# Four projections of a two-layer trunk in products of 512 columns instead of twice 256

## The chip, the core and the metric

The kernel runs on one core of a Trainium2 chip. The metric is the device time in microseconds of one execution, the median over repeated runs. The engines are called as the profile calls them: PE (matrix products), PEld (its loads of the stationary operand), DVE (vector), ACT (scalar, activation functions), POOL (GpSimd) and SP (the queue that issues the transfers). A tile is 128 partitions high; PSUM, where PE writes, has eight banks of 512 float32 columns.

## What is computed

The reference is a causal decoder trunk of two layers over 1024 positions of width 1024. Cut to what the change touches:

```python
# layer 0
proj = h @ w_in_even                       # 1024 x 3072: q, f, i, g, u, v, 512 columns each
oa = hgrn2_mix(qa, fa, ia, ga, ...)        # gated linear recurrence, then rmsnorm * silu(g)
ob = gelu(ub) * mixed(layernorm(gelu(vb))) # 128 x 128 causal mixing matrix for each chunk and group
x = x + rmsnorm(concat([oa, ob]) @ w_out_even)
x = x + rmsnorm(square(relu(rmsnorm(x) @ w_ff1)) @ w_ff2)
# layer 1
o = dilated_attention_mix(h, w_in_odd)     # 16 heads
x = x + rmsnorm(o @ w_out_odd)
x = x + rmsnorm(square(relu(rmsnorm(x) @ w_ff1)) @ w_ff2)
```

## The kernel before, in words

Every product is made of three: operands are split into a high part (rounded to the reduced float32 that PE multiplies quickly) and a low part (the rest), and high x high, high x low and low x high are summed in one PSUM bank. `HT` holds the transposed activations, high and low, as 8 blocks of 128 rows (k) by 1024 positions. `WP` is a ring of 12288 words for each partition that holds split weights.

The product in question is `gemm_nat`: for one tile t of 128 positions it takes the 8 k-blocks of `HT` as the stationary operand and streams the weights of the same k-block as the moving operand, so one call is 8 x 3 = 24 matmuls into one bank of the tag `mm`, which has three banks. Before the change the weights come in blocks of 256 columns. `gemm_tr` is the other orientation: weights stationary, 512 positions of `HT` moving.

Weights come in through `load_cols`: for each pair of k-blocks a piece is taken from HBM by SP into one of three small buffers `raw` of 128 x 512 words, ACT copies it into the high half of its place in `WP`, and DVE (in some stages POOL) subtracts to get the low half. A piece is two k-blocks of 256 columns, or one k-block of 512 columns; either way it holds 512 words for each partition.

The stages that matter here:

- Layer 0, recurrence (`hgrn`, heads 0 to 3): long chains of small DVE and ACT steps with small products of PE between them; PE fills the holes with products of later stages.
- Layer 0, block b (gMLP input, the reference's vb): the projection, a gelu of four steps (`gelu2`: ACT, DVE, ACT, DVE), a layer norm (`gmlp_norm`, many tiny DVE steps, then two products on POOL), and four small mixing products with the columns of `vn` as stationary operand (`gmlp_mix`).
- Layer 0, block u (the reference's ub): `gemm_tr` and a gelu, then a product on POOL.
- Layer 0, block g (gate): the projection, tanh, DVE and POOL steps; `onorm` normalises the recurrence's output with many DVE steps on 128 x 4 values; then each tile is transposed into `HT` (`to_HT`, `ob_to_HT`).
- Both layers, output projection (`out_and_ffn`): 8 tiles x 1024 columns. In layer 0 each tile makes all its columns in turn; in layer 1 the first three tiles begin with their first 512 columns, because the last k-block of `HT` is read back from HBM (`reload_oT`) only when the attention ends. Two of the four weight blocks of 256 columns are loaded ahead of the stage, one goes through `WP`, and one, for which `WP` has no room, into four buffers `wide` of 1024 words. The tile is then normalised (`post_part`, `post_end`, `prenorm`) and transposed for the feed-forward.

The order of instructions on each engine is fixed when the kernel is built. The program is written down as a list of operations with the data and buffers that each needs, and `Plan.run` replays it against a table of estimated costs (`cost`, `hop`, `LAG`): whenever an engine is free it takes the earliest-listed operation that is ready by these estimates. Every buffer is assigned in the same replay. So a changed shape also reorders what stands around it. On the chip each engine works through its list in order and waits where an operand isn't there.

## Time and profile before

| | |
|---|---|
| median of 3 runs | 2345.19 us (2344.57 to 2346.19) |
| profiled execution, its own time | 2341.31 us |
| its span, first to last instruction | 2339.5 us |
| PE busy | 2277.3 us (97%), 12466 matmuls |
| DVE, ACT, POOL busy | 1607.7, 1119.3, 1086.5 us |
| mean granted clock of PE | 0.993 |
| matmuls with 256 moving columns | 2688, of which 2304 are in the four projections |

PE busy is the share of the span in which at least one matmul was in the array; matmuls overlap at their ends, so the mean length of one is longer than its share of the time. How quickly a stretch of matmuls goes is read from the start of the first to the start of the next different group. Idle time of PE stands in square brackets behind a row of the timeline, with the engine whose result came last.

### The profile page before, as it was taken

Reading aid. Unit: us, or ns where it says so; the run is one execution under the profiler, and the core shown is the slowest. Engines: PE = TensorE matmul, PEld = TensorE weight load, DVE = VectorE, ACT = ScalarE, POOL = GpSimd, SP = SyncE. Lnnn points to the kernel's source line nnn. Section 1 sums busy time; section 2 is a strip of 40 time slices with the busy share of each in tenths; the row PEclk is TensorE's granted clock in tenths of the full one; section 3 lists DMA queues with packets and bytes.
Section 4 is the critical chain, followed back from the end, with each engine's and each line's share of the span. In section 5 each row is a group of like instructions: output and inputs, shape, how many; then the busy total and the mean of one; then the engine's idle time right before and its main releaser. Section 6 shows DMA issues by size and latency. Waiting matters only on the chain. (4 is left out here: it accounts for less than half of the span.)

```text
span 2339.5 us, 35350 instructions
## 1 busy us (share of the span) xinstructions
PE 2277.3 (97%) x12466; PEld 1996.2 (85%) x12466; DVE 1607.7 (69%) x3146; ACT 1119.3 (48%) x2427; POOL 1086.5 (46%) x1192
## 2 busy tenths in 40 slices
PE   8999999999999998999999999998999999999998
PEld 7888889988888787887999999997988888888887
DVE  7698785565555855848888777876665555777646
ACT  6444435452222343335777777787453222443333
POOL 2121344345555799514555555543245555644204
PEclk9999999999999999999999999999999999999999
DMA  5110114234443867755311111114334444778554
GB/s 172 55 32 24 37 37 132 82 112 168 149 155 133 287 225 250 253 193 173 100 47 46 46 46 46 52 43 140 126 109 149 154 156 140 287 272 297 200 172 161
DMA packets 220921, 319.25 MB, mean 136 GB/s; under 512 B 14132, under 2 KB 111432, under 8 KB 220744
## 3 DMA queue, kind: packets, MB, share of 16 engines
q1 hardware_dynamic: 220744, 317.00, 40.1%
q8 instruction: 98, 1.61, 0.3%
q14 instruction: 79, 0.65, 0.1%
HBM read 226.24 MB, written 90.70 MB: 135 GB/s over the span
## 5 line engine op out<-in xcount | busy, mean ns | idle before, releaser
L422 POOL TENSOR_TENSOR b<-b,b 128x512 f32<-128x512 f32 (+5 forms) x510 | 562.9, 1119 | 715.1 <-ACT b L422 357.0
L422 PE MATMUL mm<-WP,HT 128*128 128x256 f32 (+2 forms) x4704 | 835.1, 324 | 6.9 <-DVE b L422 2.9
L422 PEld LDWEIGHTS mm<-WP,HT 128*128 128x128 f32 x4704 | 713.7, 191 | 50.6 <-DVE b L422 3.3
L422 ACT ACTIVATE b<-b 128x512 f32<-128x512 f32 (+6 forms) x661 | 325.6, 508 | 372.8 <-POOL b L422 200.5
L422 POOL TENSOR_TENSOR b<-b 128x512 f32<-128x512 f32 (+4 forms) x366 | 331.1, 910 | 343.6 <-DVE b L422 233.7
L422 ACT ACTIVATE WP<-b 128x1024 fp32r<-128x1024 f32 (+2 forms) x248 | 194.8, 792 | 345.0 <-PE pb L422 189.3
L422 DVE TENSOR_TENSOR WP<-b,WP 128x1024 fp32r<-128x1024 f32 (+1 forms) x164 | 234.3, 1434 | 145.8 <-ACT WP L422 145.5
L422 DVE TENSOR_TENSOR b<-b,b 128x1024 fp32r<-128x1024 f32 (+6 forms) x371 | 240.3, 664 | 93.4 <-ACT b L422 76.7
L422 ACT ACTIVATE b<-mm 128x512 f32<-128x512 f32 (+3 forms) x362 | 155.0, 441 | 283.4 <-PE mm L422 266.0
L422 DVE TENSOR_TENSOR HT<-b,HT 128x1024 fp32r<-128x1024 f32 (+3 forms) x131 | 189.7, 1456 | 16.8 <-ACT HT L422 16.6
L422 PE MATMUL tr<-b,b 128*128 128x128 f32 x1074 | 172.3, 279 | 24.3 <-DVE b L422 20.0
L422 PE MATMUL pa<-WP,HT 128*128 128x512 f32 x768 | 193.8, 390 | 0.0
L422 DVE TENSOR_TENSOR b<-tr,b 64x128 fp32r<-64x128 f32 (+5 forms) x404 | 162.9, 408 | 33.4 <-ACT b L422 26.1
L422 PE MATMUL tr<-WP,HT 128*128 128x512 f32 x672 | 171.8, 392 | 6.9 <-DVE b L422 6.6
L422 PE MATMUL mm<-HT,b 128*128 128x512 f32 x720 | 174.8, 390 | 1.5 <-ACT b L422 1.5
L422 PE MATMUL pa<-WP,b 128*128 128x512 f32 x720 | 173.6, 389 | 0.8 <-DVE b L422 0.8
L422 ACT ACTIVATE HT<-b 128x1024 fp32r<-128x1024 f32 (+4 forms) x147 | 142.8, 973 | 62.5 <-DMA b<-hc 38.0
L422 PEld LDWEIGHTS pa<-WP,HT 128*128 128x128 f32 x768 | 144.4, 188 | 29.9
L422 PEld LDWEIGHTS tr<-b,b 128*128 128x128 f32 x1074 | 130.1, 148 | 40.5 <-DVE b L422 20.5
L422 DVE TENSOR_TENSOR b<-pa,b 128x512 f32<-128x512 f32 x110 | 75.3, 688 | 129.0 <-PE pa L422 129.0
L422 PEld LDWEIGHTS pa<-WP,b 128*128 128x128 f32 x720 | 135.0, 188 | 29.6 <-DVE b L422 1.6
L422 PEld LDWEIGHTS mm<-HT,b 128*128 128x128 f32 x720 | 134.6, 188 | 29.8 <-ACT b L422 2.3
(63 smaller groups left out, 3074.6 us busy)
## 6 DMA issues: line engine op xcount, KB each, us to landing
b<-in_w_ff_dram SPq DMA_DIRECT2D x172, 512.0 KB, 4.8
hc<-b SPq DMA_DIRECT2D x224, 256.0 KB, 2.1
b<-hc SPq DMA_DIRECT2D x112, 512.0 KB, 5.0
b<-in_w_in_odd_dram SPq DMA_DIRECT2D x64, 192.0 KB, 2.8
x<-b SPq DMA_DIRECT2D x24, 512.0 KB, 2.6
b<-x SPq DMA_DIRECT2D x24, 512.0 KB, 3.3
b<-in_w_in_even_dram SPq DMA_DIRECT2D x32, 256.0 KB, 2.9
wd<-b SPq DMA_DIRECT2D x16, 512.0 KB, 3.2
```

Source lines behind the costliest of these rows:

```text
L422: return getattr(self.real[eng], meth)(*[x.real() if isinstance(x, View) else x for x in a], **{k: x.real() if isinstance(x, View) else x ...
```

## The change

Block b, block g and both output projections are taken in products of 512 columns:

- `gemm_nat` always takes a bank and the weights as they were loaded; one call for 512 columns is 24 matmuls, where two calls of 24 made the same columns.
- Blocks b and g become one entry of the list each (width 512), so their gelu, tanh and gate steps run once on 512 columns. The row sums of the layer norm come out of one accumulation, and the addition of two halves goes.
- The weights of b and g take 8192 words of `WP` each; the next block can be loaded beside them only if it takes at most 4096.
- The output weights are cut by column half and by k: `wout[half, 0]` holds k-blocks 0 to 3 and `wout[half, 1]` holds 4 to 7, 512 columns wide. Layer 0 loads (0, 0) ahead of the stage and (0, 1) into `wide`; (1, 0) and (1, 1) go through `WP` when the gate's weights are done. Layer 1 loads (0, 0) during the last pair of heads and (0, 1) behind it; (1, 1) goes into `wide`.
- `wide` is two buffers of 2048 words instead of four of 1024. Two blocks of SBUF of that size exist.

The number of weight words, pieces and multiplications is the same.

```diff
-    def gemm_nat(self, t, w, c0, width, o=None):
-
-        if o is None:
-            o = self.mm_bank()[:, :width]
+    def gemm_nat(self, t, w, width):
+
+        o = self.mm_bank()[:, :width]
         ts = slice(t * P, (t + 1) * P)
         for k in range(NK):
-            self.mm3(o, self.HT[:, 0, k, ts], self.HT[:, 1, k, ts],
-                     w[0][k][0][:, c0:c0 + width], w[0][k][1][:, c0:c0 + width], k == 0, k == NK - 1)
+            self.mm3(o, self.HT[:, 0, k, ts], self.HT[:, 1, k, ts], *w[k], k == 0, k == NK - 1)
         return o
...
-            blocks = [("b", B0), ("b", B0 + 256), ("u", U0), ("u", U0 + 256), ("g", G0), ("g", G0 + 256)]
+            blocks = [("b", B0, 512), ("u", U0, 256), ("u", U0 + 256, 256), ("g", G0, 512)]
...
-                    self.wout = [self.load_cols(a["w_out_even"][0], [256 * i], 256) for i in range(2)]
+                    self.wout = {(0, 0): self.load_cols(a["w_out_even"][0], [0], 512, (0, 2))}
...
-                        x = self.gemm_nat(t, cur, 0, 256)
+                        x = self.gemm_nat(t, cur[0], 512)
                         if kind == "b":
-                            if half == 0:
-                                sums[t] = self.small(2)
-                            self.gelu2(pl2, vs[t][:, cs], x, accum=sums[t][:, half:half + 1])
-                            if half == 1:
-                                self.gmlp_mix(t, ob, self.gmlp_norm(pl2, vs[t], sums[t]))
+                            s = self.small()
+                            self.gelu2(pl2, vs[t], x, accum=s)
+                            self.gmlp_mix(t, ob, self.gmlp_norm(pl2, vs[t], s))
                         else:
-                            if half == 0:
-                                self.onorm(pl2, oa[t])
-                            th = pl2.tile([P, 256], F32, name="th", tag="th", bufs=2)
+                            self.onorm(pl2, oa[t])
+                            th = pl2.tile([P, 512], F32, name="th", tag="th", bufs=2)
                             nc.scalar.activation(th, x, AF.Tanh, scale=0.5)
                             nc.vector.scalar_tensor_tensor(th, th, 1.0, x, op0=OP.add, op1=OP.mult)
-                            nc.gpsimd.tensor_tensor(oa[t][:, cs], oa[t][:, cs], th, op=OP.mult)
-                            if half == 1:
-                                self.to_HT(t, [oa[t][:, k * P:(k + 1) * P] for k in range(4)], t % 2 == 1)
-                                self.ob_to_HT(t, ob)
+                            nc.gpsimd.tensor_tensor(oa[t], oa[t], th, op=OP.mult)
+                            self.to_HT(t, [oa[t][:, k * P:(k + 1) * P] for k in range(4)], t % 2 == 1)
+                            self.ob_to_HT(t, ob)
...
-                    wnext = self.load_cols_lazy(self.a["w_out_odd"][0], [0], 256)
+                    wnext = self.load_cols_lazy(self.a["w_out_odd"][0], [0], 512, (0, 2))
...
-        self.wout = [wcur, self.load_cols_lazy(self.a["w_out_odd"][0], [256], 256)]
+        self.wout = {(0, 0): wcur, (0, 1): self.load_cols_lazy(self.a["w_out_odd"][0], [0], 512, (4, 6))}
...
-            self.wout.append(self.load_cols(wo, [512], 256))
-            self.wout.append(self.load_cols(wo, [768], 256, buf=[
-                pl.tile([P, 1024], F32R, name="wide", tag=f"wide{j}", bufs=1) for j in range(4)]))
+            wide = [pl.tile([P, 2048], F32R, name="wide", tag=f"wide{j}", bufs=1) for j in range(2)]
+            for x in ((0, 0), (0, 1), (1, 0), (1, 1)):
+                if x not in self.wout:
+                    buf = wide if x == ((1, 1) if l else (0, 1)) else None
+                    self.wout[x] = self.load_cols(wo, [512 * x[0]], 512, (4 * x[1], 4 * x[1] + 2), buf)
...
-                bank = self.mm_bank()
-                for i in range(2):
-                    self.gemm_nat(t, self.wout[2 * hf + i], 0, 256, bank[:, 256 * i:256 * i + 256])
+                bank = self.gemm_nat(t, self.wout[hf, 0][0] + self.wout[hf, 1][0], 512)
```

Three places of the built order bear on the prediction. In these rows a name with a number (`b_541`) is a block of SBUF that the planner handed out, so the numbers differ between the kernels; `mm`, `tr`, `pa`, `pb` are PSUM tags.

**PE at the end of the recurrence.** `pb` rows read the recurrence out, `tr` rows with a right operand such as `b_569` are its state updates, and `mm<-WP,HT` is block b's projection. Before:

```order
L422 MATMUL tr<-b_86,b_349 128x128 x4
L422 MATMUL pb<-b_541,b_230 128x128
L422 MATMUL pb<-b_93,b_431 128x128
L422 MATMUL tr<-b_93,b_569 128x128 x2
L422 MATMUL pb<-b_686,b_230 128x128
L422 MATMUL pb<-b_93,b_431 128x128
L422 MATMUL pb<-b_686,b_230 128x128
L422 MATMUL pb<-b_94,b_431 128x128
L422 MATMUL tr<-b_94,b_569 128x128
L422 MATMUL pb<-b_541,b_230 128x128
L422 MATMUL pb<-b_94,b_431 128x128
L422 MATMUL mm<-WP,HT 128x256 x228
```

and with the change:

```order
L422 MATMUL mm<-WP,HT 128x512 x3
L422 MATMUL tr<-b_93,b_569 128x128 x2
L422 MATMUL mm<-WP,HT 128x512 x6
L422 MATMUL pb<-b_686,b_230 128x128
L422 MATMUL pb<-b_93,b_431 128x128
L422 MATMUL pb<-b_686,b_230 128x128
L422 MATMUL pb<-b_94,b_431 128x128
L422 MATMUL tr<-b_94,b_569 128x128
L422 MATMUL mm<-WP,HT 128x512 x6
L422 MATMUL pb<-b_541,b_230 128x128
L422 MATMUL pb<-b_94,b_431 128x128
L422 MATMUL mm<-WP,HT 128x512 x33
```

Block b's matmuls now stand between the recurrence's last steps; between the recurrence's last use of `WP` for its own weights and its last read-out stand 69 of 512 columns, where 72 of 256 stood.

**DVE at the end of block u.** `SCALAR_TENSOR_TENSOR` rows with `mm` are the gelu steps that free a bank, `WP<-` rows are the last step of a weight piece, 128x4 rows belong to `onorm`. Before, the gate's first four pieces end among the earlier gelus of u:

```order
L422 TENSOR_TENSOR WP<-b_87,WP 128x512
L422 SCALAR_TENSOR_TENSOR b_2733<-b_2618,mm 128x512
L422 TENSOR_SCALAR b_86<-b_86 128x4
L422 TENSOR_TENSOR b_89<-b_86,b_89 128x4
L422 TENSOR_TENSOR WP<-b_88,WP 128x512
L422 TENSOR_TENSOR b_89<-b_86 128x4
L422 TENSOR_TENSOR WP<-b_89,WP 128x512
```

With the change the last four of the gate's eight pieces stand behind the last step of u's seventh gelu (the first row) and, the eighth, behind that of its eighth (the row ahead of the last):

```order
L422 SCALAR_TENSOR_TENSOR b_2655<-b_2344,mm 128x512
L422 TENSOR_TENSOR b_94<-b_94,b_86 128x512
L422 TENSOR_TENSOR WP<-b_88,WP 128x512
L422 TENSOR_TENSOR WP<-b_89,WP 128x512
L422 TENSOR_TENSOR WP<-b_87,WP 128x512
L422 SCALAR_TENSOR_TENSOR b_2447<-b_2447,mm 128x512
L422 TENSOR_TENSOR b_86<-b_89,b_86 128x4
L422 TENSOR_TENSOR b_89<-b_86 128x4
L422 TENSOR_TENSOR b_89<-b_89,b_86 128x4
L422 TENSOR_SCALAR b_89<-b_89 128x4
L422 SCALAR_TENSOR_TENSOR b_2447<-b_2447,mm 128x512
L422 TENSOR_TENSOR WP<-b_88,WP 128x512
```

The gate's last weights are now ready only when block u's gelus are over.

**PE where layer 1's attention ends.** The last `pb` rows are the last products of the attention, `mm_74` to `mm_76` are the three banks, so a change of the number is a change of tile or column half. Before:

```order
L422 MATMUL pb_81<-b8_8892,b15_8796 128x128 x2
L422 MATMUL mm_76<-WP_67,HT_63 128x256 x9
L422 MATMUL mm_74<-WP_67,HT_63 128x256 x21
L422 MATMUL mm_75<-WP_67,HT_63 128x256 x27
L422 MATMUL mm_76<-WP_67,HT_63 128x256 x27
L422 MATMUL mm_74<-WP_67,HT_63 128x256 x27
```

and with the change:

```order
L422 MATMUL pb_81<-b1_8060,b15_7964 128x128 x2
L422 MATMUL mm_76<-WP_67,HT_63 128x512 x21
L422 MATMUL mm_75<-WP_67,HT_63 128x512 x9
L422 MATMUL mm_74<-WP_67,HT_63 128x512 x3
L422 MATMUL mm_76<-WP_67,HT_63 128x512 x3
L422 MATMUL mm_75<-WP_67,HT_63 128x512 x15
L422 MATMUL mm_74<-WP_67,HT_63 128x512 x12
```

Before, 30 matmuls of 256 columns stand between the attention's last product and the first that needs the last k-block of `HT`; now 30 of 512 columns do, and the first that needs it are the three of `mm_74`.

More of the change, by code (lines that the diff above doesn't have):

```diff
@@ L886, in layer0_mix @@
                         nxt = (self.load_cols(w, [Q0 + (h + 1) * P, F0 + (h + 1) * P], P) if h < 3
-                               else self.load_cols(w, [blocks[0][1]], 256))
+                               else self.load_cols(w, [blocks[0][1]], blocks[0][2]))
                     state = self.hgrn(ph, h, b, fps, qps, oa, state)
@@ L893, in layer0_mix @@
             pl2 = nc.pool(2)
-            pl2.reserve("gz256", 256, F32, 2)
             vs = [pl2.tile([P, 512], F32, name="vs", bufs=NT) for t in range(NT)]
             ob = [[pl.tile([P, 2, 512], F32, name=f"ob{i}{j}") for j in range(2)] for i in range(2)]
-            sums = {}
-            for n, (kind, c0) in enumerate(blocks):
+            for n, (kind, c0, width) in enumerate(blocks):
                 nxt = None
                 if n + 1 < len(blocks):
-                    nxt = self.load_cols(w, [blocks[n + 1][1]], 256)
+                    nxt = self.load_cols(w, [blocks[n + 1][1]], blocks[n + 1][2])
                 else:
-                    self.wout = [self.load_cols(a["w_out_even"][0], [256 * i], 256) for i in range(2)]
-                half = n % 2
-                cs = slice(half * 256, half * 256 + 256)
-                if n == 2:
+                    self.wout = {(0, 0): self.load_cols(a["w_out_even"][0], [0], 512, (0, 2))}
+                if n == 1:
                     pl2.__exit__()
@@ L914, in layer0_mix @@
                             self.gelu2(pl2, u, x)
-                            o = ob[hf][half][:, j]
+                            o = ob[hf][n - 1][:, j]
                             nc.gpsimd.tensor_tensor(o, o, u, op=OP.mult)
@@ L962, in gmlp_norm @@
         mu = self.small(nm="mu")
-        nc.vector.tensor_tensor(mu, sums[:, 0:1], sums[:, 1:2], op=OP.add)
-        nc.vector.tensor_scalar(mu, mu, -1.0 / 512, None, op0=OP.mult)
+        nc.vector.tensor_scalar(mu, sums, -1.0 / 512, None, op0=OP.mult)
         vn = pool.tile([P, 512], F32, name="vn", tag="vn", bufs=3)
@@ L1187, in qkv_stream @@
         self.rawp = self.cp, "raw", 3, [[nc.vector], [nc.vector, nc.gpsimd], [nc.vector, nc.vector, nc.gpsimd], [nc.gpsimd]][LAG["tail"]]
-        self.wout = [wcur, self.load_cols_lazy(self.a["w_out_odd"][0], [256], 256)]
-        for x in self.wout:
+        self.wout = {(0, 0): wcur, (0, 1): self.load_cols_lazy(self.a["w_out_odd"][0], [0], 512, (4, 6))}
+        for x in self.wout.values():
             for _ in x[2]:
@@ L1406, in out_and_ffn @@
                         next(weights0, None)
-            self.wfree(*self.wout[:3])
+            self.wfree(*self.wout.values())
         self.rawp = self.cp, "raw", 3, [nc.vector]
```

2 lines of the change are left out of this document (1 added, 1 removed).

## The prediction

> **What bounds the kernel now.** I read the page's first part, then the instruction groups by shape, then the timeline of PE, and last the table of stretches where PE pauses.
>
> ```profile
> PE 2277.3 (97%) x12466; PEld 1996.2 (85%) x12466; DVE 1607.7 (69%) x3146; ACT 1119.3 (48%) x2427; POOL 1086.5 (46%) x1192
> ...
> L422 PE MATMUL mm<-WP,HT 128*128 128x256 f32 x2304 | 300.9, 288 | 6.4 <-DVE b L422 2.9 <-ACT HT L422 1.5 <-DVE HT L422 1.4
> ...
> L422 PE MATMUL mm<-b,HT 128*128 128x256 f32 x384 | 50.4, 285 | 0.0
> ```
>
> PE is busy for 97% of the span, so its own work sets the time nearly everywhere, and only 62 us in all are left to pauses. The 256-column matmuls number 2304 + 384 = 2688. Of these 2 x 8 x 24 = 384 belong to layer 0's value input, which stays as it is. The other 2304 are what the change touches: 384 each in blocks b and g, 768 in each output projection. The means of 288 and 285 ns can't be used as a price, because neighbouring matmuls overlap; the price is the time from start to start:
>
> ```profile
> 232.25 27.61 PE L422 MATMUL mm<-WP,HT 128*128 128x256 f32 x228 [1.63 <-DVE b L422]
> 259.70 1.06 PE L422 MATMUL tr<-b,b 128*128 128x128 f32 x8
> ...
> 296.38 29.53 PE L422 MATMUL mm<-HT,WP 128*128 128x512 f32 x129
> 325.75 5.91 PE L422 MATMUL mm<-WP,HT 128*128 128x256 f32 x48
> 332.96 23.30 PE L422 MATMUL mm<-WP,HT 128*128 128x256 f32 x192 [1.30 <-DVE b L422]
> 356.11 0.60 PE L422 MATMUL tr<-b,b 128*128 128x128 f32 x4
> ...
> 1762.79 2.88 PE L422 MATMUL pa<-WP,b 128*128 128x512 f32 x12
> 1765.51 2.88 PE L422 MATMUL pb<-WP,b 128*128 128x512 f32 x12
> ```
>
> 256 columns: (259.70 - 232.25)/228 = 120.4 ns and (356.11 - 332.96)/192 = 120.6 ns. 512 columns: (325.75 - 296.38)/129 = 227.7 ns and (1765.51 - 1762.79)/12 = 226.7 ns. Twice the columns cost 1.89 times as much, so a fixed part of about 14 ns goes with each matmul.
>
> **The matmuls (term 1).** 2304 matmuls of 256 columns become 1152 of 512. Each pair gains 2 x 120.5 - 227.2 = 13.8 ns, together 1152 x 13.8 = 15.9 us: 5.3 in blocks b and g (384 pairs), 10.6 in the output projections (768 pairs). With the one or the other 512-column row the term is 15.3 or 16.5 us. For the output projection the table of stretches (busy us and instructions of PE, PEld, DVE, ACT, POOL, then granted clock and DMA) has
>
> ```profile
> 395.00:495.00 100.00, 100.00 (x782) 96.80 (x781) 58.84 (x121) 43.56 (x112) 31.17 (x23) 1.00 0.23 84
> ```
>
> PE without a pause and DVE at 59%: nothing else comes near, so the 10.6 us should arrive whole.
>
> The Trainium skill ("TensorE: Matmul & The Clock Gate", section "Back-to-back issue gap") gives a warm gap of N/2.4 + 2.5 ns, which speaks against the change: by it a pair would gain 2.5 ns, and my estimate from it is 1152 x 2.5 = 2.9 us. The rows above have a fixed part five times that size, and the measurement decides.
>
> **The pauses of layer 0's blocks (term 2).** The same table:
>
> ```profile
> 206.50:233.00 26.50, 22.10 (x169) 20.25 (x168) 20.49 (x60) 10.22 (x33) 2.60 (x2) 1.00 0.09 27
> 233.00:260.00 27.00, 27.00 (x227) 27.00 (x227) 15.05 (x60) 10.84 (x26) 2.59 (x2) 1.00 0.13 39
> 260.00:310.00 50.00, 46.25 (x270) 39.86 (x270) 49.09 (x192) 24.99 (x89) 25.80 (x20) 1.00 0.13 39
> 310.00:336.00 26.00, 24.70 (x144) 21.77 (x143) 25.86 (x88) 9.37 (x28) 13.94 (x11) 1.00 0.16 51
> ```
>
> PE pauses 4.40 us at the end of the recurrence, nothing in the first half of b, 3.75 in b's second half and u, and 1.30 at the third group of g: 9.45 us. The reason is the third column. While b's first half is multiplied DVE is 56% busy, because only the gelu can be done; with the second half the layer norm and the mixing come on top and DVE is 98 to 99% busy until 336 us.
>
> The change spreads this. A bank now holds 24 matmuls of 512 columns, so the three `mm` banks hold 16 us of filler for the recurrence's end instead of 8.7. In the order 69 matmuls of 512 stand where 72 of 256 stood, 15.7 us instead of 8.7; the 7 us more are work moved forward into the holes. And each tile's layer norm can begin after its one projection, from the start of b.
>
> Whether DVE keeps up decides how much is kept:
>
> ```profile
> L422 DVE SCALAR_TENSOR_TENSOR b<-b,mm 128x256 f32<-128x256 f32 x31 | 12.8, 416 | 10.4 <-ACT b L422 10.2
> L422 DVE SCALAR_TENSOR_TENSOR b<-b,mm 128x512 f32<-128x512 f32 x16 | 10.8, 678 | 0.1
> L422 DVE TENSOR_TENSOR b<-b 128x4 f32<-128x4 f32 x46 | 10.8, 248 | 0.1
> L422 DVE TENSOR_TENSOR b<-b,b 128x4 f32<-128x4 f32 x26 | 8.1, 322 | 0.0
> L422 DVE TENSOR_TENSOR b<-b 128x1 f32<-128x1 f32 x23 | 7.9, 351 | 0.2
> ```
>
> DVE's work from 233 to 336 us is 15.05 + 49.09 + 25.86 = 90 us. Block b's 32 gelu steps of 416 ns become 16 of 678, which takes off 32 x 416 - 16 x 678 = 2.5 us; about 87 are left. By the order the first gelu steps stand ahead of the recurrence's last state updates, so they start at about 230 us, and DVE is through with u at about 317 if it never waits. PE for itself would start g at 325.75 - 4.40 - 3.75 - 192 x 0.0138 = 315 us. It needs the gate's last weight piece 21 matmuls later, at 315 + 21 x 0.227 = 319.8; that piece stands in DVE's order behind u's last gelu step, so it comes at about 318. The two meet with 2 us to spare. The third group of g, which had to wait before, now starts at 315 + 48 x 0.227 = 326, long after its bank is free.
>
> I take 3 us of pauses left (the mixing products that wait for POOL, and short gaps in the recurrence) and so a gain of 6.5 us. Bounds: all 9.45 gone; or DVE 6 us later than above, which puts about 4 us of waiting at the gate's weights beside the old pauses at the recurrence, 3 more than before on balance.
>
> **Layer 1's entry into the output projection (term 3).**
>
> ```profile
> 1606.55 4.01 PE L422 MATMUL mm<-WP,HT 128*128 128x256 f32 x30
> 1612.06 14.55 PE L422 MATMUL mm<-WP,HT 128*128 128x256 f32 x105 [1.50 <-ACT HT L422]
> 1629.32 3.04 PE L422 MATMUL mm<-WP,HT 128*128 128x256 f32 x24
> ...
> 1637.96 2.68 PE L422 MATMUL mm<-b,HT 128*128 128x256 f32 x21
> 1642.83 0.74 PE L422 MATMUL tr<-b,b 128*128 128x128 f32 x4 [2.19 <-DVE b L422]
> ```
>
> After the attention's last product 30 matmuls cover the way of the last k-block into `HT`, 5.5 us, and PE waits 1.50. The 30 are now twice as wide, 6.8 us, so this wait should go but for some tenths at the second tile. The wait of 2.19 us is different: the first tile's last matmul ends at 1629.3, its transposes start at 1642.83, so its normalisation takes 13.5 us. Between the two stand 93 matmuls of 256 columns now and 51 of 512 then, 11.2 and 11.6 us: it gets 0.4 us shorter. I take 1.5 us together; bounds 0 and 3.69.
>
> **Weights that come later.** In layer 0 eight pieces instead of four go through `WP` after the gate is done. Their pace before:
>
> ```profile
> 381.41 0.63 ACT L422 ACTIVATE b<-b 128x512 fp32r<-128x512 f32 x1 [2.25 <-DMA b<-in_w_out_even_dram]
> 383.41 0.63 ACT L422 ACTIVATE b<-b 128x512 fp32r<-128x512 f32 x1 [0.88 <-DMA b<-in_w_out_even_dram]
> 385.25 0.63 ACT L422 ACTIVATE b<-b 128x512 fp32r<-128x512 f32 x1 [0.15 <-DMA b<-in_w_out_even_dram]
> 386.21 0.63 ACT L422 ACTIVATE b<-b 128x512 fp32r<-128x512 f32 x1 [0.33 <-DMA b<-in_w_out_even_dram]
> ```
>
> (386.21 - 381.41)/3 = 1.6 us each, 2.0 at worst. Three wait in the `raw` buffers and go in as the gate's k-blocks come free, the third some 2.7 us before the gate's last matmul; the other five take 8 to 10 us, so the last is there 7 to 9 us after that matmul, counting ACT and DVE. PE needs it after the first column half (24 x 0.227 = 5.4) and seven eighths of the second (4.8), 10.2 us after. Cost nothing, cover 1 to 3 us; without the cover it costs what is missing, up to 3 us. The two large `wide` buffers hold the same four pieces as the four small ones. In layer 1 the first of them is needed 63 matmuls of 512 columns after the attention's last product, 14.3 us, where it was 135 of 256, 16.3 us; PE didn't wait for it, so it costs 0 to 2 us, and I take 0. In the feed-forward I put nothing.
>
> **The sum.** 15.9 + 6.5 + 1.5 = 23.9 us off the profiled execution's own 2341.31 us is 2317.4. The median of the runs shown, 2345.19, is 3.9 above that execution, so the forecast for the median is 2321.
>
> **The rivals.**
>
> *The pauses stay.* DVE ran at 98 to 99% where PE paused, and its work hardly falls; it may only be shifted. Against it: 12 us of DVE idle in 233 to 260 become usable. Time: 2345.2 - 15.9 = 2329, and 2332 to 2334 if the gate's weights come 3 to 5 us late.
>
> *DVE eats all of layer 0's part.* Only the output projections gain: 2345.2 - 10.6 = 2334.6, up to 2340 with more waiting at u. It needs DVE 8 us or more behind my 317.
>
> *Slower: DVE and POOL in each other's way.* The same small operation takes 0.15 or 1.25 us:
>
> ```profile
> 304.34 1.25 DVE L422 TENSOR_TENSOR b<-b 128x4 f32<-128x4 f32 x1
> ...
> 306.72 0.15 DVE L422 TENSOR_TENSOR b<-b 128x4 f32<-128x4 f32 x1
> ```
>
> It happens while POOL works. The layer norms now run beside POOL from b's first tile on. Today's extra over 0.15 in the three groups of 46, 26 and 23 above is 4.5 + 4.5 + 4.6 = 13.6 us. If all 95 waited 1.1 us, 104 us, DVE would end u at 317 + 91 = 408 and the third group of g would start 82 us late: 2403. It turns the change into a loss (over 2349.9) once DVE ends u after 354.5, 0.4 us more on each of the 95. POOL's work is the same as before, which speaks against it. The Trainium skill ("SBUF — State Buffer", section "Who interferes with whom") says that a DVE instruction with two SBUF inputs contends with a POOL instruction that reads SBUF; these rows agree.
>
> *The change doesn't do what it says.* If the fixed part went with the columns, 512 would cost 241 ns and nothing would be gained; with a fixed part of 2.5 ns the gain is 2.9 us, 2342. The rows with 129 and 12 matmuls speak against both.
>
> **How the numbers follow.** Chances: the forecast (2316 to 2327) 0.55; the pauses stay (2327 to 2334) 0.27; DVE eats layer 0's part (2334 to 2340) 0.08; below 2316, with nearly all pauses gone, 0.05; no fixed part gained 0.03; slower 0.02. A measurement of this kernel can tell about 0.2%, 4.7 us, from no change; so faster 0.95, same 0.03, slower 0.02. The range 2315 to 2332 holds the forecast, the upper bounds of terms 2 and 3 short of their last 2 us, and most of the first rival.
>
> **What would show it.** Right: 512-column groups of `mm<-WP,HT` at 227 ns from start to start, 10.9 us of products for one tile of an output projection (48 x 0.227; 96 x 0.1205 = 11.6 before), no PE pause at the third group of g, DVE near 90% busy from the first tiles of b on, less than 4 us of PE pauses between the recurrence's end and g's end, no wait of 1.50 us in layer 1. Wrong: a pause of several us at g's first group (weights) or at u's groups (banks), waits of the first output tile for weights, or new pauses in the feed-forward, where I expect no difference.

## The result and the profile after

The changed kernel takes 2320.35 us (median of 4 executions, 2318.44 to 2320.78) where the kernel before took 2344.88 (median of 4, 2340.43 to 2346.19): ratio 0.9901, 95% interval [0.9889, 0.9913]. Timed once more later it took 2319.14 us (2317.92 to 2319.7) beside 2342.86 of the kernel before: 0.9893 [0.9878, 0.9909]. The forecast was 2321.0. In the four later comparisons the kernel before had medians of 2342.35, 2342.72, 2342.86 and 2343.83, so the 2345.19 that the forecast started from lay high, and the gain is 22 to 25 us.

The profiled execution has a span of 2318.9 us (2339.5 before), an own time of 2320.68, and a mean clock of 0.995. The page's first part and the instruction group by shape that the change made:

```profile
PE 2259.9 (97%) x11314; PEld 1929.9 (83%) x11314; DVE 1616.1 (70%) x3106; ACT 1114.1 (48%) x2403; POOL 1097.3 (47%) x1184
...
L422 PE MATMUL mm<-WP,HT 128*128 128x512 f32 x1824 | 455.5, 394 | 1.7 <-DVE b L422 1.2 <-DVE HT L422 0.5
```

1152 matmuls fewer, and DVE, ACT and POOL nearly as before. That the total came out right says little about the terms, so here is the same point of the program in both PE timelines (start of the named row, us):

| point | before | after | gained in the stage |
|---|---|---|---|
| last gate and query products of the recurrence | 205.03 | 203.70 | 1.33 |
| first product of block g | 325.75 | 314.91 | 9.51 |
| first product of layer 0's feed-forward | 475.21 | 463.57 | 0.80 |
| first transposes of layer 1's normalisation | 1079.87 | 1065.63 | 2.60 |
| last product of the attention | 1605.26 | 1591.35 | -0.33 |
| first product of layer 1's feed-forward | 1708.42 | 1689.40 | 5.11 |
| end of the last matmul | 2332.00 | 2311.05 | 1.93 |

The first 1.33 us are not the change: PE's first instruction stands at 9.37 us before and 8.24 after, and executions of these kernels differ there by about a microsecond. The other rows come from one execution of each kernel. In a second profiled execution of the changed kernel (e11 below) the same stages differ from these by 0.0, 0.2, 0.6, 0.3, 0.7 and 0.0 us, so a few tenths mean nothing. Block b and u gained what was forecast; the gate and layer 0's projection together, where 9.25 us were expected (2.65 + 5.3 of products and the pause of 1.30), gained 0.80; and both feed-forwards, where nothing was expected, gained 4.5.

**Block b to block g.** The PE timeline after, where g begins:

```profile
314.91 9.68 PE L422 MATMUL mm<-WP,HT 128*128 128x512 f32 x42
327.60 0.66 PE L422 MATMUL tr<-b,b 128*128 128x128 f32 x4 [3.00 <-POOL b L422]
328.01 7.33 PE L422 MATMUL mm<-WP,HT 128*128 128x512 f32 x24
...
335.53 5.73 PE L422 MATMUL mm<-WP,HT 128*128 128x512 f32 x24
```

and the table of stretches from the recurrence's end to g (busy us and instructions of PE, PEld, DVE, ACT, POOL, then granted clock and DMA):

```profile
205.00:231.50 26.50, 26.01 (x152) 22.20 (x151) 20.57 (x57) 9.60 (x27) 2.57 (x2) 1.00 0.10 29
231.50:268.80 37.30, 35.80 (x184) 29.09 (x183) 31.61 (x121) 15.79 (x41) 15.81 (x12) 1.00 0.03 8
268.80:315.00 46.20, 45.81 (x210) 37.74 (x209) 46.20 (x174) 24.81 (x86) 21.55 (x17) 1.00 0.25 74
```

At the recurrence's end 0.49 us of pause are left of 4.40, in b and u 1.50 + 0.39 of 3.75. DVE is 85% busy in b and has no gap in u. The stage's gain of 9.51 us is 2.65 of products and 5.77 of pauses (8.15 before, 2.38 after); the remaining 1.1 us are not accounted for. Then there are two things that the kernel before did not have: PE waits 3.00 us for POOL ahead of the gate's first transposes, and the 24 matmuls behind them take 7.33 us, while the next 24 take 5.73. The clock says why. Microsecond by microsecond, after the pause:

```profile
328.00:329.00 1.00, 1.00 (x7) 0.87 (x6) 1.00 (x3) 0.60 (x1) 0.16 (x1) 0.95 0.00 0
329.00:330.00 1.00, 1.00 (x4) 0.69 (x4) 0.97 (x2) 0.00 (x0) 1.00 (x1) 0.50 0.64 225
...
332.00:333.00 1.00, 1.00 (x5) 0.78 (x5) 0.00 (x0) 0.00 (x0) 1.00 (x1) 0.84 0.81 227
```

The granted clock (third number from the right) drops to 0.50, for the three microseconds from 329 to 332: 0.05 + 3 x 0.50 + 0.16 = 1.7 us are lost after the pause, on top of it.

**Layer 0's output projection**, the transposes of four neighbouring tiles in the PE timeline, without the products between them:

```profile
411.53 0.66 PE L422 MATMUL tr<-b,b 128*128 128x128 f32 x4 [0.75 <-DVE b L422]
...
424.30 0.66 PE L422 MATMUL tr<-b,b 128*128 128x128 f32 x4 [0.75 <-DVE b L422]
...
435.70 1.03 PE L422 MATMUL tr<-b,b 128*128 128x128 f32 x8
...
447.48 1.04 PE L422 MATMUL tr<-b,b 128*128 128x128 f32 x8
```

The undisturbed tile takes 447.48 - 435.70 = 11.78 us (12.38 before); three tiles take 12.76, because DVE ends the tile's normalisation 0.75 us late. DVE's last step of it is a pair of 512-element multiplications. Its timeline, and POOL's, in a tile that waits and in one that doesn't:

```profile
408.98 2.49 DVE L422 SCALAR_TENSOR_TENSOR b<-b,b,b 128x512 f32<-128x512 f32 x2
...
434.51 1.42 DVE L422 SCALAR_TENSOR_TENSOR b<-b,b,b 128x512 f32<-128x512 f32 x2
```

```profile
409.65 1.27 POOL L422 TENSOR_TENSOR b<-b,b 128x512 f32<-128x512 f32 x1 [4.15 <-ACT b L422]
...
435.24 3.08 POOL L422 TENSOR_TENSOR b<-b,b 128x512 f32<-128x512 f32 x2 [4.22 <-ACT b L422]
```

The pair takes 2.49 us where POOL's operation on the next column half begins inside it and is through first, and 1.42 where POOL is the one that takes longer. Before, the pair took 1.41 to 1.42 us in these tiles (407.18, 419.56). So 1.07 us are lost to the two engines in each other's way. Which of them waits hangs on little: POOL's operation begins 0.67 us into the pair in the slow tile and 0.73 us into it in the other. This is read from the trace; no run takes POOL's operation away.

**Layer 1's entry** lost its wait at the last k-block but got others; and where the kernel before waited 1.50 us, its clock fell too. The PE timeline after, and then two of the stretches behind that wait before:

```profile
1624.89 1.42 PE L422 MATMUL tr<-b,b 128*128 128x128 f32 x8 [3.45 <-DVE b L422]
...
1642.48 0.66 PE L422 MATMUL tr<-b,b 128*128 128x128 f32 x4 [0.93 <-DVE b L422]
...
1661.90 0.66 PE L422 MATMUL tr<-b,b 128*128 128x128 f32 x4 [0.75 <-DVE b L422]
```

```profile
1612.00:1613.00 1.00, 0.94 (x4) 0.82 (x5) 0.39 (x1) 0.00 (x1) 0.00 (x0) 0.77 0.75 215
1613.00:1614.00 1.00, 1.00 (x7) 1.00 (x6) 0.05 (x1) 0.71 (x2) 0.00 (x0) 0.50 0.94 277
```

From 1612 to 1617 us the granted clock before was 0.77, 0.50, 0.50, 0.52 and 1.00: in this execution that wait cost 1.50 + 1.7 us. After the change the first tile's transposes wait 3.45 us for DVE. Here are the 15 us ahead of them, in which that tile is normalised, and the 20 us behind:

```profile
1610.00:1625.00 15.00, 11.55 (x52) 9.26 (x51) 10.72 (x21) 11.51 (x23) 2.93 (x2) 1.00 0.47 145
1625.00:1645.00 20.00, 19.07 (x87) 15.32 (x88) 19.12 (x37) 13.32 (x31) 5.17 (x3) 0.91 0.43 146
```

DVE is 71% and ACT 77% busy ahead of the transposes, and DVE 96% behind them. Both also write the reloaded halves into `HT` there, between the steps of the normalisation, so what the transposes wait for looks like a chain over two engines and not like DVE at its limit.

**The feed-forward's first weights.** SyncE's queue before and after:

```profile
467.11 12.72 SPq L422 DMA_DIRECT2D x<-b  x2
...
496.26 0.94 SPq L422 DMA_DIRECT2D b<-in_w_ff_dram  x2
```

```profile
456.77 2.30 SPq L422 DMA_DIRECT2D b<-in_w_ff_dram  x4
```

The first loads into `ff1`'s landing buffers `R` are issued at 496.3 us before and 456.8 after. The blocks that the planner gives the buffers in the built kernels suggest why; e2 and e3 below test it. `R` needs blocks of 2048 words, and there are two. Four `wide` buffers of 1024 words go into small blocks; `ff1`'s first weights (`unit0`, 4 x 1024 words) are then put into the two large ones, and `R` waits until they are used up. Two `wide` buffers of 2048 take the large blocks, `unit0` goes elsewhere, and `R` follows `wide`, which in layer 0 is free after the last tile's first column half. Three PE waits are gone after the change, in layer 0 and alike in layer 1; these are the rows before:

```profile
508.74 3.01 PE L422 MATMUL mm<-HT,b 128*128 128x512 f32 x12 [0.74 <-ACT b L422]
...
514.70 2.60 PE L422 MATMUL pa<-WP,b 128*128 128x512 f32 x10 [0.45 <-DVE b L422]
...
524.73 3.02 PE L422 MATMUL pa<-HT,b 128*128 128x512 f32 x12 [0.63 <-DVE b L422]
```

### The profile page after: what moved, and what is told of

The parts are those of the page before. It is cut to its first block, busy times and chain, and to the rows that moved or that the text cites. A ratio compares the mean times of both kernels' runs of the same rounds, so it can differ in the third digit from the quotient of the medians.

```text
span 2318.9 us, 32947 instructions
## 1 busy us (share of the span) xinstructions
PE 2259.9 (97%) x11314; PEld 1929.9 (83%) x11314; DVE 1616.1 (70%) x3106; ACT 1114.1 (48%) x2403; POOL 1097.3 (47%) x1184
## 4 chain that ended last, share of the span: by engine, by line
PE 75%; DVE 12%; ACT 4%; POOL 3%; DMA 3%; issue 2%; SPq 0%; DVEq 0%; ACTq 0%; POOLq 0%
PE mm L422 34%; PE pa L422 20%; PE pb L422 13%; PE tr L422 9%; DVE b L422 9%; POOL b L422 3%; ACT b L422 3%; DVE WP L422 2%; DVE HT L422 1%; DMA b<-in_w_ff_dram 1%; DMA b<-in_w_in_odd_dram 1%; DMA b<-oTd 1%; DMA b<-hc 1%; ACT HT L422 0%; ACT WP L422 0%
## 5 line engine op out<-in xcount | busy, mean ns | idle before, releaser
L422 POOL TENSOR_TENSOR b<-b,b 128x512 f32<-128x512 f32 (+4 forms) x500 | 576.4, 1169 | 668.3 <-ACT b L422 324.5
L422 PE MATMUL mm<-WP,HT 128*128 128x512 f32 (+2 forms) x3744 | 822.5, 362 | 3.3 <-DVE HT L422 1.2
L422 PEld LDWEIGHTS mm<-WP,HT 128*128 128x128 f32 x3744 | 655.3, 190 | 82.1 <-DVE HT L422 2.3
L422 DVE TENSOR_TENSOR WP<-b,WP 128x1024 fp32r<-128x1024 f32 (+1 forms) x164 | 225.8, 1385 | 127.9 <-ACT WP L422 127.5
L422 DVE TENSOR_TENSOR HT<-b,HT 128x1024 fp32r<-128x1024 f32 (+3 forms) x131 | 217.9, 1671 | 23.2 <-ACT HT L422 23.0
```

The costliest lines, as they stand in the source:

```text
L422: return getattr(self.real[eng], meth)(*[x.real() if isinstance(x, View) else x for x in a], **{k: x.real() if isinstance(x, View) else x ...
```

## The experiments

All times are medians; "the changed kernel" stands for 2320.35 us. The kernel before took 2342.35 us beside the first four runs, 2342.72 beside the next four, 2342.86 beside the next three and 2343.83 beside the last. Rows are from the PE timeline where nothing else is said.

**Two halves for each matmul (e1).** In `gemm_nat`:

```diff
-            self.mm3(o, self.HT[:, 0, k, ts], self.HT[:, 1, k, ts], *w[k], k == 0, k == NK - 1)
+            for c in range(0, width, 256):
+                self.chain3(o[:, c:c + 256], self.HT[:, 0, k, ts], self.HT[:, 1, k, ts],
+                            w[k][0][:, c:c + 256], w[k][1][:, c:c + 256],
+                            k == 0 and c == 0, k == NK - 1 and c == width - 256)
```

> The changed kernel (2320.35 us) with each of its 1152 matmuls of 512 columns issued as two of 256 columns on the same weights, banks and order of tiles; the result is the same. Theory (a fixed part of 13.8 ns goes with each matmul): 1152 x 13.8 = 15.9 us come back on PE, less up to 3 us of them where PE now waits for the first gate tile and for three output tiles, so 2333 to 2336 us; two neighbouring 256-column matmuls 241 ns from start to start. Block b stays ordered tile by tile, so the pauses at the recurrence's end and in b stay gone. Rival 1 (a fixed part of 2.5 ns): 2323 us. Rival 2 (the pauses went because of the width itself): they come back, 2342 us.

Measured: 2331.91 us (2330.5 to 2333.2), 11.6 more than the changed kernel. Layer 0's projection:

```profile
440.71 0.60 PE L422 MATMUL tr<-b,b 128*128 128x128 f32 x4
...
453.11 0.60 PE L422 MATMUL tr<-b,b 128*128 128x128 f32 x4
```

A tile takes 12.40 us again, 0.62 more than the undisturbed 11.78, which is 12.9 ns for each of its 48 pairs. Layer 1's projection costs 4.82 us more (12.6 ns for each of 384 pairs), though PE's waits in it are 0.4 us shorter; without that it would be about 13.7 ns. So the fixed part goes with the matmul and is about what the prediction said; a fixed part of 2.5 ns would have given 0.12 us per tile. The total came out 1 us under the range. No tile of layer 0 waits for DVE now, which the range allowed for, and the pauses up to block g got shorter too. They did not return: from the last gate and query products to block g PE pauses 1.7 us (2.4 in the changed kernel, 8.2 before), and the stretch is only 1.3 us longer than in the changed kernel. Wide matmuls are not what removed them.

**Block b in two column passes again (e5).** `blocks` begins with `("b", B0, 256), ("b", B0 + 256, 256)`, with the sums and the layer norm split as before.

> The changed kernel with block b back at twice 256 columns, the first column half over all tiles and then the second, as before; u, g and both output projections as changed. Theory (the pauses went because each tile's layer norm now follows its one projection, from the start of b): the pauses at the recurrence's end and in b's second half and u come back, 8.15 us where the changed kernel has 2.3, and the products cost 192 x 13.8 ns = 2.6 more; the gate starts 8 to 9 us later and the time is 2328 to 2330 us. Rival (the pauses went because three banks hold 16 us of filler): the filler is halved, but DVE's order alone is not decisive, 2323 to 2325 us.

Measured: 2328.4 us (2326.99 to 2331.43). Block g:

```profile
323.54 9.68 PE L422 MATMUL mm<-WP,HT 128*128 128x512 f32 x42
336.57 1.11 PE L422 MATMUL tr<-b,b 128*128 128x128 f32 x4 [3.35 <-POOL b L422]
```

The gate starts 8.63 us later than in the changed kernel, as the theory said, and the first waits of b and u are those of the kernel before (1.07, 0.48, 0.92 us). Counted from the last gate and query products of the recurrence and set beside e1: 256 columns tile by tile cost the gate's start 1.3 us, 256 columns in two passes 8.3. So it is not the width. The order of the tiles, by which each layer norm follows its one projection, and the longer filler that three banks hold then, both come back with e5 and both stay with e1; these runs don't tell the two apart.

**The gate in two passes again (e4).** `blocks` ends with `("g", G0, 256), ("g", G0 + 256, 256)`, with tanh, gate steps and transposes split as before.

> The changed kernel with block g back at twice 256 columns, all else as changed. Products: 192 x 13.8 ns = 2.6 us more. Theory 1 (the wait of 3.00 us at the gate's first transposes and the 1.6 us behind it come from asking for a tile's transposes at once, and two passes of 256 give DVE and POOL 23 us to get there): 4.6 us less, 2318.4 us in all. Theory 2 (DVE comes out of block u at 318 us and is late whatever stands next, so the wait moves to the fourth group of g, which needs a bank that DVE frees at about 325): the wait stays 2 to 4 us, 2321 to 2323 us.

Measured: 2319.76 us (2318.28 to 2320.6), no difference from the changed kernel.

```profile
316.00 5.91 PE L422 MATMUL mm<-WP,HT 128*128 128x256 f32 x48
322.16 23.30 PE L422 MATMUL mm<-WP,HT 128*128 128x256 f32 x192 [0.26 <-DVE b L422]
```

The wait of 3.00 us and the half clock behind it are gone, and what is left in their place is 0.26. From g to the feed-forward the kernel is 0.99 us faster than the changed one: 4.6 for the pause less 2.65 for the products and one more of the 0.98 us tiles. So in block g the change won nothing: what the wide matmuls gained went into a pause that the single pass had opened.

**The gate's transposes two tiles later (e6).** Shortened; the two tiles left in `late` are transposed behind the loop.

```diff
                         x = self.gemm_nat(t, cur[0], 512)
+                        if len(late) == 2:
+                            self.to_HT(*late.pop(0))
...
-                            self.to_HT(t, [...], t % 2 == 1)
+                            late.append((t, [...], t % 2 == 1))
```

> The changed kernel with one thing moved: in block g a tile's transposes stand two tiles later in the program, so PE has 72 matmuls of 512 columns (16.3 us) ahead of the first of them instead of 42 (9.5 us). Theory (the 3.00 us wait and the 1.6 us lost behind it are a wait for the gate's first product on POOL, which ends at 327.5 us): both go, 4.6 us less, 2315.8 us. Rival (DVE and POOL are late in any case, so PE waits for the bank of the first tile at the fourth, or for the output projection's first weights): 2319 to 2320 us.

Measured: 2317.23 us (2315.43 to 2317.67).

```profile
315.44 16.49 PE L422 MATMUL mm<-WP,HT 128*128 128x512 f32 x72
331.76 0.60 PE L422 MATMUL tr<-b,b 128*128 128x128 f32 x4
```

No pause and no half clock; the stage from g to the feed-forward is 4.42 us shorter (4.6 expected). Of these, 3.7 are left at the end of the profiled execution and 3.1 in the median. Against the changed kernel's second measurement (2319.14 us) it is 1.9 in the median. As ratios to the kernel before, the two intervals overlap (0.9891 [0.9878, 0.9905] and 0.9901 [0.9889, 0.9913]), so the gain is clear in the stage and not in the total.

**Large extra buffers alone (e2).** In the kernel before:

```diff
-            self.wout.append(self.load_cols(wo, [768], 256, buf=[
-                pl.tile([P, 1024], F32R, name="wide", tag=f"wide{j}", bufs=1) for j in range(4)]))
+            wide = [pl.tile([P, 2048], F32R, name="wide", tag=f"wide{j}", bufs=1) for j in range(2)]
+            self.wout.append(self.load_cols(wo, [768], 256, buf=[x[:, i:i + 1024] for x in wide for i in (0, 1024)]))
```

> The kernel before (2344.88 us) with one thing of the change alone: the projection's four extra weight pieces lie in two buffers of 2048 words instead of four of 1024. No matmul changes. Theory (found in the two traces, not in the prediction): the feed-forward's landing buffers R need blocks of 2048 words, of which there are two; with small extra buffers the feed-forward's first weights sit there and the first R load is issued at 496 us, while with large ones R follows the extra weights and is loaded some 20 us earlier. The PE waits of 0.74, 0.45, 0.63 us (layer 0) and 0.74, 0.34, 0.63 us (layer 1) behind the feed-forward's start go: 3.5 to 4 us, so 2341 us. Rival (the waits come from DVE and ACT being busy, the loads have nothing to do with it; the prediction's own view): no change, 2345 us.

Measured: 2342.5 us, ratio 0.9998 [0.9989, 1.0007]. The six waits did go: the stage from layer 0's feed-forward to layer 1 is 3.74 us shorter, from layer 1's feed-forward to the end 2.63. But layer 1's output projection became 5.0 us longer:

```profile
1612.16 14.53 PE L422 MATMUL mm<-WP,HT 128*128 128x256 f32 x105 [3.52 <-ACT HT L422]
...
1644.55 1.97 PE L422 MATMUL tr<-b,b 128*128 128x128 f32 x8 [3.47 <-DVE b L422]
```

Both waits were there before, with 1.50 and 2.19 us. A new one of 0.51 us stands at 1605.92, and behind the second the clock is 0.50 for about seven microseconds instead of three, which is 1.4 us more. R's loads moved as the theory said, from 496.26 to 474.47 us in layer 0 and from 1729.51 to 1709.49 in layer 1. The mechanism was right and the time was not: it was lost at another place, which I hadn't priced. In layer 1 the large blocks hold the attention's last buffers; that the extra weights come later for that reason was not tried by itself.

**Four small buffers in the changed kernel (e3).**

```diff
-            wide = [pl.tile([P, 2048], F32R, name="wide", tag=f"wide{j}", bufs=1) for j in range(2)]
+            wide = [pl.tile([P, 1024], F32R, name="wide", tag=f"wide{j}", bufs=1) for j in range(4)]
```

(each k-block's high and low half then lie in one of them).

> The changed kernel with the extra weights in four buffers of 1024 words again, all else as changed. Theory (early R loads are worth 3.5 to 4 us): the waits behind the start of both feed-forwards come back, 2324 us. Rival (the size of the buffers is worth nothing, as predicted): 2320.4 us. A wait of the first output tile of layer 0 for weights is possible beside it, since the small blocks come free later: up to 2 us more.

Measured: 2321.79 us (2319.78 to 2322.05), 1.4 more, about as much as two measurements of the changed kernel differ (2320.35 and 2319.14). The waits returned in both layers:

```profile
497.38 3.01 PE L422 MATMUL mm<-HT,b 128*128 128x512 f32 x12 [0.69 <-ACT b L422]
...
1722.59 3.01 PE L422 MATMUL mm<-HT,b 128*128 128x512 f32 x12 [0.74 <-ACT b L422]
```

From layer 1's feed-forward to the end it takes 1.78 us more, as the theory wants. Layer 0's projection also waits 0.23 and 0.73 us for weights at 376 and 378 us, as the expectation had allowed. Layer 0's feed-forward is 2.28 us behind after its first 400 matmuls and has made it up by layer 1: in the second half of the feed-forward PE waits in every one of these kernels, mostly for DVE, 1.85 + 7.30 + 1.20 us in the changed kernel and 0.53 + 2.70 + 2.35 + 1.38 here. Why that stall got shorter I did not find. By the traces the large buffers are worth 1 to 2 us here, less than the forecast of this run; the medians don't tell that from the 0 of the prediction.

**The projections' transposes later (e7), and both (e8).** Behind two column halves in layer 0 and three in layer 1 (shortened; `turn_in` does what the line taken out and the two behind it did):

```diff
                 bank = self.gemm_nat(t, self.wout[hf, 0][0] + self.wout[hf, 1][0], 512)
+                late = [x - 1 for x in late]
+                if late and late[0] <= 0:
+                    late.pop(0)
+                    turn_in(done.pop(0))
...
-                    self.h_to_HT(t, ys[t])    # and ff1_sums, weights0
+                    late.append(3 if l else 2)
+                    done.append(t)
```

> The changed kernel with the transposes of a finished tile of the output projections moved later: behind two column halves of the next work in layer 0 (48 matmuls, 10.9 us, where 33 stand now) and behind three in layer 1 (72, 16.3 us, where 51 stand). Theory (the waits of 0.75 us in layer 0, each with some 0.2 us beside it, and of 3.45, 0.93 and 0.75 us in layer 1 are the normalisation of a tile being 8 and 15 us long): they go, 2.9 + 5.1 us, 2312.3 us. Rival (the wait only moves to the feed-forward, whose sums of two tiles come later): 2317 to 2320 us.

Measured: 2322.03 us (2318.89 to 2322.4). The rival was right:

```profile
401.73 1.03 PE L422 MATMUL tr<-b,b 128*128 128x128 f32 x8
413.50 1.04 PE L422 MATMUL tr<-b,b 128*128 128x128 f32 x8
...
474.69 0.66 PE L422 MATMUL tr<-b,b 128*128 128x128 f32 x4 [0.51 <-DVE HT L422]
...
1639.16 1.97 PE L422 MATMUL tr<-b,b 128*128 128x128 f32 x8 [5.45 <-DVE HT L422]
```

In layer 0 every tile now takes 11.8 us and the projection is 3.08 us shorter, but the feed-forward, whose first transposes come out of the sums of tiles 6 and 7, is 3.04 longer. In layer 1 the wait moved some 13 us back and grew: 72 matmuls and not 51 stand ahead of it, and PE still waits for DVE.

> The changed kernel with the transposes moved later in block g (two tiles) and in both output projections (two and three column halves). Theory: the gains add, 4.6 + 8.0 us, 2307.7 us, faster than both kernels. Rival (what is gained is waited for in the feed-forward, where PE has pauses of some 10 us for DVE already): 2313 to 2318 us.

Measured: 2317.12 us (2315.49 to 2318.6), the same as with the late gate alone.

**Only tiles 0 to 4 of layer 0 later (e9), and the reload on POOL (e10).** e9 is e6 with e7's late list for tiles 0 to 4 of layer 0 alone (`if l or t > 4: turn_in(t)`, else two column halves later); e10 adds one line in `reload_oT`:

```diff
-        (nc.gpsimd if t < LAG["rel"] else nc.vector).tensor_tensor(lo, src, hi.bitcast(F32), op=OP.subtract)
+        (nc.gpsimd if t >= 4 else nc.vector).tensor_tensor(lo, src, hi.bitcast(F32), op=OP.subtract)
```

> The changed kernel with the gate's transposes two tiles later (the edit that gave 3.1 us) and, in layer 0's output projection alone, the transposes of tiles 0 to 4 later by two column halves; tiles 5 to 7, whose sums the feed-forward waits for, and layer 1 stay as changed. Theory (the 3 us that the late transposes of both layers gained in layer 0 were lost again in the feed-forward because tile 6 was late, not because of tiles 0 to 4): 2.9 us less than with the late gate alone, 2314.3 us. Rival (the feed-forward's stalls take back whatever reaches it earlier): 2317 us.

> The kernel of the run before this one, with the low halves of the attention's output of tiles 4 to 7 written to HT by POOL instead of DVE (8 operations of 128x512, 1.1 us each on DVE) where layer 1's projection begins. Theory (the wait of 3.45 us at the first tile's transposes, which only moved when PE was given more work ahead of it, is DVE's throughput there, 96% busy from 1625 to 1645 us): 8.8 us of DVE work leave, the wait falls by 2 to 3 us, 2311 to 2312 us. Rival (POOL's reads slow the DVE operations beside them, or the late tiles reach HT too late for the product): no gain or a loss, 2314 to 2318 us.

> The changed kernel itself once more, on the same chip as the two runs beside it, for a direct comparison: 2318.4 to 2320.8 us if its time holds.

Measured side by side: the changed kernel 2319.14 us (2317.92 to 2319.7), e9 2313.34 (2312.55 to 2314.14), e10 2312.06 (2311.15 to 2313.4; against the kernel before 0.9864 [0.9849, 0.988]). e9 is 5.8 us faster than the changed kernel; in the traces it is 4.4 us in the gate and 3 in layer 0's tiles, with 1 lost again in the feed-forward. So most of what the late transposes of e7 lost came from the last tiles, not from tiles 0 to 4. In e10 the first tile's transposes, and behind them one stretch as in the tables above:

```profile
1617.34 1.42 PE L422 MATMUL tr<-b,b 128*128 128x128 f32 x8 [2.66 <-DVE b L422]
```

```profile
1617.00:1637.00 20.00, 19.65 (x89) 15.85 (x90) 16.66 (x34) 12.67 (x30) 9.91 (x6) 0.91 0.48 161
```

DVE is 83% busy in the 20 us behind the first tile, 16.66 us where the same stretch of e9 has 19.12. The wait fell from 3.43 to 2.66 us and the stage by 1.25, half of what was expected, and the medians of e9 and e10 are too close to tell them apart. The theory's 96% were measured behind the wait; in the 15 us ahead of it DVE is 72% busy in e9. And its rival is partly there: in e10 a DVE pair ahead of the first tile's transposes takes 2.74 us at 1606.55, beside POOL's writes to `HT`, where it took 1.41 in the changed kernel (1617.00).

**Four leading tiles in layer 1 (e12),** on top of e10: `n = 4 * l` for `3 * l`, and tile 3 among the early reloads.

> The kernel of the run before (late gate, late tiles 0 to 4 of layer 0's projection, reload of tiles 4 to 7 on POOL) with four tiles instead of three in the leading group of layer 1's output projection: the first column half of tiles 0 to 3, then the second half of tiles 0 to 3, and tile 3's attention output reloaded with those of tiles 0 to 2. Theory (the wait of 2.66 us at the first tile's transposes is one tile's normalisation of some 15 us against 51 matmuls, 11.6 us, and after it the granted clock is 0.5 for about 3.5 us, which costs 1.7 us more): 75 matmuls, 17.0 us, cover it, both go, 4.3 us less, 2307.8 us. Rival 1 (DVE has no room there, so the wait only moves to a later tile): no gain, 2312 us. Rival 2 (the clock is half for another reason than the pause): 2.7 us less, 2309.4 us, the clock still 0.5 somewhere near.

Measured: 2315.72 us (2313.89 to 2316.67), or 0.9878 [0.9862, 0.9895] of the kernel before, where e10 had 0.9864 [0.9849, 0.988]. The 4.3 us did not come; that it is slower than e10 is not clear from the totals, but layer 1's output projection takes 2.6 us longer in the trace.

```profile
1600.37 0.73 PE L422 MATMUL mm<-WP,HT 128*128 128x512 f32 x2 [2.35 <-ACT HT L422]
...
1627.95 0.66 PE L422 MATMUL tr<-b,b 128*128 128x128 f32 x4 [1.09 <-DVE b L422]
```

The wait at the transposes shrank to 1.09 us, with no fall of the clock behind it (1.00 from 1608 on). But with one more tile to reload the last k-blocks reach `HT` later, and there a new wait of 2.35 us stands, with a clock of 0.79 over the next 8 us, which is 1.7 us on top of it. It is the rival of a moved wait, at a place that neither rival named.

## Why the prediction came out right

**Term 1, the matmuls (15.9 us).** Right. e1 gives 12.6 to 13.7 ns for each pair in the projections where 13.8 was read off the timeline. The Trainium skill's fixed part of 2.5 ns ("TensorE: Matmul & The Clock Gate", section "Back-to-back issue gap") would have made e1 2.9 us slower; it was 11.6. The section gives that gap for an isolated matmul and says that in a stream of weight loads and matmuls both set the spacing, so the prediction set the formula against a case that it isn't meant for. What failed is the sentence after the table of stretches, that in the output projection "nothing else comes near, so the 10.6 us should arrive whole". DVE's mean of 59% hid a chain: a tile's transposes stand 33 matmuls, 7.5 us, after its last product, and in three tiles POOL now ran into the end of the normalisation. 3 x 0.98 us went there. It is the mechanism of the rival in which DVE and POOL are in each other's way, at a place where it was not looked for and at a price of 1.07 us a tile.

**Term 2, the pauses of layer 0 (gain 6.5).** The first part was right, reason and size: from the recurrence's end to the gate 9.51 us were gained, of which 2.65 are products and 5.77 pauses, and the gate began at 314.91 where 315 was said (1.1 us of that came with the earlier start). e1 and e5 show that the change of passes did it and not the width; of its two reasons in the prediction, layer norms that begin with the first tile and 16 us of filler, neither is shown alone. The second part failed, at the step "the third group of g ... now starts at 315 + 48 x 0.227 = 326, long after its bank is free". It asked for banks and weights and not for the next wait in line, the first tile's transposes, which the change puts right behind the first tile: before, the whole first column pass stood ahead of them. PE came to them after 42 matmuls, at 324.6, and POOL's product was there at 327.5. So the sign "less than 4 us of PE pauses between the recurrence's end and g's end" failed, with 5.4 us and 1.7 more at half clock; e4 and e6, which both put more matmuls ahead of the first transposes, took the pause away.

A misreading is part of it. The four `WP` rows that were given as the gate's last weights are the output projection's first ones:

```profile
294.88 3.66 SPq L422 DMA_DIRECT2D b<-in_w_out_even_dram  x3
```

```profile
315.26 4.09 DVE L422 TENSOR_TENSOR WP<-b,WP 128x512 fp32r<-128x512 f32 x3
...
320.71 0.69 DVE L422 SCALAR_TENSOR_TENSOR b<-b,mm 128x512 f32<-128x512 f32 x1
```

The gate's weights were complete at 298 us, so the "2 us to spare" were never at stake, and block u's end did not decide when they came; but these pieces stand ahead of u's last gelu step, which DVE reached at 320.7 and not at 317, and ahead of the first tile of the gate. The names in the order are those of the tiles, and `WP` is the same for all weights: which DMA filled the source has to be looked up.

**Term 3, layer 1's entry (gain 1.5).** The wait of 1.50 went as said, and had cost 3.2 with the clock behind it. The wait at the first tile's transposes, expected 0.4 shorter, grew from 2.19 to 3.45: the step "its normalisation takes 13.5 us" took the old length as given, and it took 15. The reason is open. While it runs, DVE is 71% and ACT 77% busy, both with the reload's halves too, and with eight low halves taken off DVE (e10) 0.77 us of the wait went and not the 2 to 3 expected. Together with two tiles that wait 0.93 and 0.75 us the stage gained 5.11, of which 5.3 are the products; 6.8 were expected.

**Buffers and the feed-forward ("I put nothing").** Wrong in its parts: 2.6 and 1.9 us were gained there. The prediction followed how much the buffers hold and not which blocks they take, and what has to go elsewhere for that. By e2 and e3 the large buffers are worth 0 in the one kernel and 1.4 us, hardly more than the noise, in the other, since other waits take the gain back.

**The sum.** 23.9 us were forecast for the profiled execution: 10.75 to the gate, 9.25 to the feed-forward and 6.8 in layer 1, less 3 allowed for left pauses. Its span fell by 20.6. The misses were 1.2, 8.45 and 1.7 us in that order; 4.5 from the feed-forwards and 1.3 from the start came in. Then the 3.9 us between the profiled execution of before and its median were carried over to the changed kernel, whose profiled execution (2320.68) lies at its median: without that the forecast would have been 3.3 us too low. The range held, but the agreement of 2321 with 2320 is luck in good part.

## What to carry to other kernels

When PE's work over a chain of other engines gets shorter, compare that chain with the work over it tile by tile: a mean busy share of 59% doesn't show that a tile's normalisation can run into POOL's next operation and end 0.75 us late. Where a loop of two passes becomes one, look for what stood behind the first pass (here a tile's transposes) and say what it will wait for; moving it two tiles back in the program took 4.4 us off the stage and 2 to 3 off the time, and with the same edit in the first tiles of the projection 5.8. When buffers change size, follow where the allocator puts the others.

## What the hardware showed that was not expected

A short pause of PE can cost more than itself. After the pauses of 1.50 and 2.19 us (before), 3.00 us (after) and 2.35 us (e12) the granted clock was 0.50 for about three microseconds, some 1.7 us each; after one of 3.47 us in e2 it was 0.50 for about seven. But the length of the pause doesn't decide it. In the kernel after, one of 1.74 us at 1575 us, and before, one of 1.63 at 232, had no such effect, with the clock at 1.00 in every microsecond around them. In the second profiled execution of the changed kernel (e11) the same pause, 1.75 us at 1574.61, was followed by a clock of 0.50 in 1581 and 1582, some five microseconds later. And in e1 a pause of 3.37 us ending at 1072.04 had no effect, where the kernel after, with the same pause of 3.37 us ending at 1065.63, fell to 0.50. So from these runs no length can be given from which it happens, and a fall of the clock that one execution shows may be missing in another of the same kernel. The Trainium skill ("TensorE: Matmul & The Clock Gate", section "What's actually happening") has the clock halved after an idle window of about 3.4 us and back after as long a busy one. The way back agrees with the rows of about three microseconds; the way down does not, since a pause of 1.50 us was enough here. A pause in the profile should be priced with the clock of the microseconds behind it, in more than one execution.
